# Low parts of 16 weight chunks made by ScalarE and an adding transfer, in one transformer layer

## The chip, the cores and the metric

The kernel runs on one core of a Trainium2 chip. The metric is device microseconds of one execution. A core has TensorE (PE, with its weight loads PEld), VectorE (DVE), ScalarE (ACT), GpSimd (POOL) and SyncE (SP), which run side by side and wait for one another by semaphores, and 16 DMA engines that all of them share. Each engine works through its own instructions in order; so do the queues from which SyncE, ScalarE and GpSimd issue transfers.

## The reference

One layer over a sequence of 256 tokens of width 2048, all in float32: an adaptive scale and shift, windowed attention, a norm, and an MLP of inner width 8192 with another scale, shift and norm. What matters here is the MLP:

```python
u = jnp.square(jax.nn.relu(h @ w1 + b1))
return u @ w2 + b2
```

`w1` is 2048 x 8192 and `w2` 8192 x 2048. The reference multiplies in float32.

## The kernel before

**Split matmuls.** TensorE multiplies in a shorter format (float32r). To keep the accuracy, weights and activations are each split in a high part (the value rounded to that format) and a low part (the value less its high part), and most products are made of three matmuls: high by high, high by low, low by high (`mm3`, lines 543 to 546; line 545 is the one that reads the weight's low part).

**Weights.** A planner (`Stream`) has a list of chunks of 128 x 2048 floats (1 MB). `loads` (line 210) issues their loads from SyncE, in the order of the list, each as soon as one of five `raw` buffers is free. `pump` then makes each chunk's two halves of 128 x 1024 ready, in order: ScalarE casts the raw half to the high part (`wh`, line 277, five buffers), and VectorE subtracts that from the raw half for the low part (`wl`, line 230 in `low`, five buffers). The low parts run one half behind the high parts. When the last low part of a chunk is made, its raw buffer is given back (`freed`), and TensorE's use of a half gives back its `wh` and `wl` (`done`). A chunk with a `use` of its own (the gates) is not split.

**The MLP in four blocks** of 2048 inner columns. In block 0, all of `w2` goes through `ff_out`, one 512-wide output column `c` after the other. In blocks 1 to 3, `ff_mixed` alternates `hidden` (a 128-wide piece of `w1`, activation on ScalarE and VectorE at lines 989 to 996) with `chunk` (output columns 0 and 1 by a product scheme with fewer multiplications, which needs sums of weights and of activations; the latter are `sc`, lines 1004 to 1009). Output columns 2 and 3 then follow in `ff_out`: per column four chunks of `w2`, that is eight halves, each read by twelve matmuls. So in blocks 1 and 2 sixteen halves go through `ff_out` in a row. Beside them VectorE adds up the scheme's results (`gather`, line 1115) and the columns (line 1181) and rescales the residual (`rescale`, lines 1154 and 1155) with rows that GpSimd loads (`gb`, line 1151). Those loads, the gathered column `w`, and the small tiles of the activation share four buffers.

**Order.** In this part of the kernel a scheduler places each engine's instructions, following the order in which the code issues them and when their inputs come free.

Of the kernel before, what the change touches and what calls it, by code (L numbers as in the profile page):

```python
# [14 lines left out]
AF = mybir.ActivationFunctionType  # L15
OP = mybir.AluOpType
# [4 lines left out]
S = 256  # L21
# [27 lines left out]
def hybrid_kernel(ctx: ExitStack, tc: tile.TileContext, a, out: bass.AP):  # L49
    nc = tc.nc  # L50
# [26 lines left out]
    def f32(x):  # L77
        return x.bitcast(F32)
# [97 lines left out]
    class Stream:  # L176
# [4 lines left out]
        def __init__(self):  # L181
            self.q, self.raw = [], []
            self.hs, self.ls, self.src = [], [], []
            self.free, self.home, self.used = [raws] * RAWS + [raws2] * MORE, [], 0
            self.of = []
            self.deep = True
            self.at = self.im = 0
            self.nh, self.nl = NHIGH, NLOW
            self.stop = 0
            self.pace = VECS  # L190
            self.pin = self.behind = False
            self.prev = None
            self.side = {}
            self.parts, self.total, self.j = [], 0, 0
            self.reserve = 0

        def plan(self, src, use=None, kept=0):
            self.q.append((src, use, kept))
            if use is None:
                n = 4 if kept < 0 else 2  # L200
                self.parts.append((self.total, n))
                self.total += n
# [21 lines left out]
        def low(self):  # L224
            n = len(self.ls)
            r, kept, l, last = self.src[n]
            w = r.shape[-1]
            if l is None:
                l = (g4, g4b)[kept - 1](F32R) if kept > 0 else wlp.tile([128, 1024], F32R, name="wl")
            self.pinned(nc.vector.tensor_sub(l[:, :w], r, f32(self.hs[n])[:, :w]))  # L230
            self.ls.append(l)
            if last:
                self.freed(self.of[n])
# [15 lines left out]
        def pump(self, vecs, must=0):  # L249

            while len(self.ls) < must or self.at < len(self.q):
                self.loads()
                n = len(self.hs)
                if len(self.ls) < n - 1 and len(self.ls) - self.used < self.nl or len(self.ls) < min(must, n):
                    self.low()
                    continue
                if self.at >= len(self.q) or self.at == self.stop:
                    return
                assert self.at < len(self.raw)
                src, use, kept = self.q[self.at]  # L260
                if use is not None:
                    if not vecs and n >= must:
                        return
                    vecs = max(vecs - 1, 0)
                    use(self.raw[self.at])
                    self.at += 1
                    self.freed(self.at - 1)
                    continue
                if n >= must and (n - self.used >= self.nh or kept > 0):
                    return  # L270
                j, raw, l = self.j, self.raw[self.at], None
                if kept < 0:
                    h, s, l = self.sums(raw, j)
                else:
                    h = (g4, g4b)[kept - 1](F32R) if kept else whp.tile([128, 1024], F32R, name="wh")
                    s = raw[:, j * 1024:j * 1024 + 1024]
                self.pinned(nc.scalar.copy(h[:, :s.shape[-1]], s))  # L277
                self.hs.append(h)
                self.src.append((s, kept, l, j == (3 if kept < 0 else 1)))
                self.of.append(self.at)  # L280
                self.j = (j + 1) % (4 if kept < 0 else 2)
                self.at += self.j == 0
# [30 lines left out]
    S = Stream()  # L313
# [155 lines left out]
    for g in range(2, G):  # L469
        n = len(ORDER[g])  # L470
# [43 lines left out]
    def plan_out(blk, c):  # L514
        for kg in range(4):
            if blk < BLK - 1:
                m_gf.plan(gf_fill.pop(0))
            S.plan(a["w2"][4 * min(blk, 1) + 2 * max(blk - 1, 0) + (c if blk == 0 else c - 2), kg], None,
                   max(kg - 1, 0) if blk == BLK - 1 and c == 3 else 0)

    first_gf = len(S.q)
    for c in range(4):
        plan_out(0, c)
    for blk in range(1, BLK):
        w1 = [a["w1b"][(blk - 1) * NF + f] for f in range(NF)]
        S.plan(w1[0])
        S.plan(w1[1])
        for i in range(NP):
            if i + 1 < NP:
                S.plan(w1[2 * i + 2])  # L530
            S.plan(a["w2s"][blk - 1, i], None, -1)
            if i + 1 < NP:
                S.plan(w1[2 * i + 3])
        for c in (2, 3):
            plan_out(blk, c)
# [73 lines left out]
    def qkv(g, ch):  # L609

        _, k0, nk = m_mix[g]
        hh, hl = held[g]
        wh, wl = S.main()
        per = 4 // nk
        for ci in range(per):
            p = ch * per + ci
            c = CORD[p]
            go_on, held_back = c in half, ((g, ch), p) in CARRY
            pss = half.pop(c, None) or banks()
            for k2 in range(0, nk, 2):  # L620
                for t in range(NT):
                    for k in (k2, k2 + 1):
                        s = slice(k * 256 + t * 128, k * 256 + t * 128 + 128)
                        mm3(pss[t], hh[:, s], hl[:, s], wh(ci * nk + k), wl(ci * nk + k),
                            k == 0 and not go_on, k == nk - 1 and not held_back)
                S.done()
                if per == 1 and k2 == 0:
                    yield
            if held_back:
                half[c] = pss  # L630
            else:
                evict(c, pss)
            if per == 2 and ci == 0:
                yield
# [36 lines left out]
    for x, (g, c) in enumerate(qk_order):  # L671
        at = ORDER[g].index(c)
# [157 lines left out]
    def project(j, c):  # L830
        wh, wl = S.main()
        oh, ol = oT[j]
        pss = [psa.tile([128, 512], F32, name="pa") for _ in range(NT)]
        last = j == 3 and c == 3
        for t, rs in [(0, range(4)), (1, range(4))] if last else [(t, (r, r + 1)) for r in (0, 2) for t in range(NT)]:
            for r in rs:
                s = slice(t * 512 + r * 128, t * 512 + r * 128 + 128)
                mm3(pss[t], oh[:, s], ol[:, s], wh(r), wl(r), r == 0, r == 3)
            if t == 1 or last:
                S.done(not last)  # L840
            if last:
                add_gated(pss[t], t, c, g1, st)
                sc.append(norm_scalars(st[t]))
                normed(0, t)
            if t == 1 and rs[0] == 0:
                yield
        for t, ps in enumerate(pss):
            if j == 0:
                nc.vector.tensor_add(part(ys, t, c), ps, bo(c))
            elif j < 3:  # L850
                y = part(ys, t, c)
                nc.vector.tensor_add(y, y, ps)
                if j == 2:
                    z = part(xs, t, c)
                    nc.vector.tensor_mul(y, y, g1(c))
                    nc.vector.scalar_tensor_tensor(z, z, ALPHA, y, op0=OP.mult, op1=OP.add)
            elif not last:
                add_gated(ps, t, c, g1, st)
# [21 lines left out]
    for n in range(21):  # L880
        j, i = n // 4, n % 4
# [9 lines left out]
        if n + 1 < len(LATE):  # L891
            w = qkv(*LATE[n + 1])
        else:
            if n == 5:
                ys, bo = [g4b() for _ in range(4)], bias_all(a["bo"], [g4b(), g4b()])
            w = project((n - 5) // 4, (n - 5) % 4)
# [13 lines left out]
        if n == 9:  # L910

            for c in range(4):
                xs[c] = g4()
                i = nc.gpsimd.dma_start(xs[c].rearrange("p (t n) -> p t n", t=NT), a["x"][:, :, 512 * c:512 * c + 512])
# [101 lines left out]
    for n, (kg, fq) in enumerate(W1A):  # L1016
# [4 lines left out]
        for fp in range(2):  # L1021
# [3 lines left out]
            for fi in range(2):  # L1025
                o = ps[:, fi * 256:fi * 256 + 256]
                for k in range(4):
                    w = (fp * 2 + fi) * 4 + k
# [158 lines left out]
    blk = BLK - 1  # L1187
# [130 lines left out]
```

## Time and profile before

| | us |
|---|---|
| median of the runs shown | 1081.9 |
| lowest and highest of 2 | 1081.1, 1082.71 |
| profiled execution | 1085.78 |
| its span | 1084.0 |
| PE busy in it | 1051.5 |
| DVE busy | 926.1 |
| ACT busy | 611.3 |
| POOL busy | 31.0 |

The transfers move 292.70 MB, at a mean of 270 GB/s; 10.50 MB of them go through GpSimd's software queue:

```profile
q1 hardware_dynamic: 39312, 279.85, 66.4%
q0 software_dynamic: 3232, 10.50, 2.8%
```

The columns are packets, MB, and the time that the packets took as a share of 16 engines' span. In the rows of the timeline quoted below stand the start in us, the length, engine, line, operation, output and inputs, and in brackets how long the engine stood idle before and what ended that.

### The profile page before, as it was taken

To read this page: it belongs to the slowest core of one execution; us is meant where nothing else is said; L and a number is where in the kernel's file an instruction comes from. 1 tells how busy PE (TensorE), PEld (TensorE's weight loads), DVE (VectorE), ACT (ScalarE), POOL (GpSimd) and SP (SyncE) were. 2 spreads that over 40 slices of the span, in tenths; PEclk is the share of its full clock that TensorE was granted. 3 is DMA by queue.
4 is the path that set the end of the run, shared out by engine and by line. 5 is a ranking of instruction groups with operands and counts; after the bars stand their busy time and mean duration, and the time that the engine had idled before them with its cause. 6 is when DMAs were issued, how large, how long until landed. Compare 5 with 4: busy or idle time off the path is not lost.

```text
span 1084.0 us, 15688 instructions
## 1 busy us (share of the span) xinstructions
PE 1051.5 (97%) x6026; PEld 846.6 (78%) x6026; DVE 926.1 (85%) x1371; ACT 611.3 (56%) x977; POOL 31.0 (3%) x56
## 2 busy tenths in 40 slices
PE   7899999999999999999999999999999999999995
PEld 5567677666677799988888888888888888888884
DVE  5497899978899877998769889869988977998897
ACT  5333346775773636654357766447767536776640
POOL 1000000001000000000000000000000001000001
PEclk9999999999999999999999999999999999999998
DMA  9999997779976797699835644944564773556632
GB/s 384 426 425 428 425 376 286 277 282 383 368 291 233 322 352 294 236 337 408 342 116 195 215 173 159 385 156 158 192 226 172 273 277 141 183 204 219 246 156 77
DMA packets 43371, 292.70 MB, mean 270 GB/s; under 512 B 5136, under 2 KB 5264, under 8 KB 9504
## 3 DMA queue, kind: packets, MB, share of 16 engines
q1 hardware_dynamic: 39312, 279.85, 66.4%
q0 software_dynamic: 3232, 10.50, 2.8%
q10 hardware_dynamic: 752, 1.35, 0.3%
q8 instruction: 47, 0.77, 0.3%
q14 instruction: 28, 0.23, 0.1%
HBM read 289.57 MB, written 2.11 MB: 269 GB/s over the span
## 4 chain that ended last, share of the span: by engine, by line
PE 81%; DVE 9%; DMA 7%; ACT 2%; issue 1%; SPq 0%; DVEq 0%; ACTq 0%
PE pa L1060 17%; PE pa L544 12%; PE pa L546 12%; PE pa L545 12%; PE pa L1062 8%; DMA raw<-in_modm 4%; PE pa L1033 3%; PE pa L1032 3%; PE pa L1034 3%; DVE wl L230 3%; PE pm L340 2%; DVE g L378 2%; DMA raw<-in_wqkv 1%; DMA raw<-in_modf 1%; PE pa L733 1%
## 5 line engine op out<-in xcount | busy, mean ns | idle before, releaser
L277 ACT CAST wh<-raw 128x1024 fp32r<-128x1024 f32 (+1 forms) x332 | 335.5, 1020 | 288.8 <-PE pa L546 143.6
L230 DVE TENSOR_TENSOR wl<-raw,wh 128x1024 fp32r<-128x1024 f32 (+1 forms) x332 | 387.8, 1181 | 77.0 <-ACT wh L277 71.5
L544 PE MATMUL pa<-wh,g 128*128 128x512 f32 x648 | 258.4, 399 | 5.2 <-ACT g L565 2.1
L546 PE MATMUL pa<-wh,g 128*128 128x512 f32 x648 | 252.8, 393 | 3.7 <-DVE g L567 3.0
L545 PE MATMUL pa<-wl,g 128*128 128x512 f32 x648 | 254.5, 393 | 0.3 <-DVE wl L230 0.3
L1060 PE MATMUL pa<-g,wh 128*128 128x512 f32 x768 | 193.5, 393 | 0.0
L1060 PEld LDWEIGHTS pa<-g,wh 128*128 128x128 f32 x768 | 139.6, 188 | 32.0 <-DVE rl L990 4.5
L544 PEld LDWEIGHTS pa<-wh,g 128*128 128x128 f32 x648 | 121.9, 188 | 41.2 <-issue 7.8
L546 PEld LDWEIGHTS pa<-wh,g 128*128 128x128 f32 x648 | 121.8, 188 | 34.5 <-DVE g L567 6.0
L545 PEld LDWEIGHTS pa<-wl,g 128*128 128x128 f32 x648 | 122.2, 189 | 26.8 <-issue 2.2
L1062 PEld LDWEIGHTS pa<-g,wl 128*128 128x128 f32 x768 | 104.7, 190 | 7.6
L1062 PE MATMUL pa<-g,wl 128*128 128x256 f32 x768 | 107.0, 282 | 0.0
L378 DVE SCALAR_TENSOR_TENSOR g<-raw,cact,g 128x1024 f32<-128x1024 f32 x65 | 82.5, 1278 | 2.4 <-DMA raw<-in_modf 1.9
L1033 PE MATMUL pa<-g,wh 128*128 128x256 f32 x256 | 72.7, 285 | 0.4 <-DVE g L961 0.4
L1032 PE MATMUL pa<-g,wh 128*128 128x256 f32 x256 | 72.5, 286 | 0.0
L1034 PE MATMUL pa<-g,wl 128*128 128x256 f32 x256 | 72.3, 283 | 0.0
L230 DVE TENSOR_TENSOR raw<-raw 128x1024 fp32r<-128x1024 f32 x48 | 58.5, 1221 | 8.6 <-ACT raw L277 7.0
L277 ACT CAST raw<-raw 128x1024 fp32r<-128x1024 f32 x48 | 50.6, 1054 | 13.2 <-PE pm L546 9.8
L340 PE MATMUL pm<-raw,cact 128*32 128x256 f32 (+2 forms) x776 | 47.3, 365 | 8.0 <-DMA raw<-in_modm 4.6
L1032 PEld LDWEIGHTS pa<-g,wh 128*128 128x128 f32 x256 | 48.8, 192 | 1.3 <-issue 0.8
L1033 PEld LDWEIGHTS pa<-g,wh 128*128 128x128 f32 x256 | 49.1, 192 | 0.9 <-DVE g L961 0.8
L1034 PEld LDWEIGHTS pa<-g,wl 128*128 128x128 f32 x256 | 49.1, 192 | 0.0
(220 smaller groups left out, 1205.9 us busy)
## 6 DMA issues: line engine op xcount, KB each, us to landing
raw<-in_w1b SPq DMA_DIRECT2D x48, 1024.0 KB, 5.5
raw<-in_w SPq DMA_DIRECT2D x40, 1024.0 KB, 8.3
raw<-in_modm SPq DMA_DIRECT2D x32, 1024.0 KB, 14.5
raw<-in_modf SPq DMA_DIRECT2D x32, 1024.0 KB, 6.8
raw<-in_wqkv SPq DMA_DIRECT2D x24, 1024.0 KB, 14.1
raw<-in_w2s SPq DMA_DIRECT2D x24, 1024.0 KB, 4.7
raw<-in_modgm SPq DMA_DIRECT2D x16, 1024.0 KB, 7.6
raw<-in_wo SPq DMA_DIRECT2D x16, 1024.0 KB, 7.9
```

The lines of the kernel that those rows point to most:

```text
L230: self.pinned(nc.vector.tensor_sub(l[:, :w], r, f32(self.hs[n])[:, :w]))
L277: self.pinned(nc.scalar.copy(h[:, :s.shape[-1]], s))
L340: i = nc.tensor.matmul(self.ps[32 * j:32 * j + 32, :w], lhsT[j] if type(lhsT) is list else lhsT, rhs[j], start=self.first, stop=stop)
L378: nc.vector.scalar_tensor_tensor(p[:, :e], s, cact[:, kt:kt + 1], p[:, :e], op0=OP.mult, op1=OP.add)
L544: nc.tensor.matmul(ps, xh, wh, start=start, stop=False)
L545: nc.tensor.matmul(ps, xh, wl, start=False, stop=False)
L546: S.prev = nc.tensor.matmul(ps, xl, wh, start=False, stop=stop).ins
L1032: nc.tensor.matmul(o, wh(w, 128), hh, start=new, stop=False)
L1033: nc.tensor.matmul(o, wh(w, 128), hl, start=False, stop=False)
L1034: nc.tensor.matmul(o, wl(w, 128), hh, start=False, stop=end)
L1060: nc.tensor.matmul(ps, wh(k, 128), ff_in(k), start=k == 0, stop=False)
L1062: nc.tensor.matmul(ps[:, :256], wl(k, 128), ff_in(k)[:, :256], start=False, stop=k == NK - 1)
```

## The change

For the chunks of `w2` that blocks 1 and 2 send through `ff_out` (8 each, 16 chunks, 32 halves) the low part is no longer made by VectorE. ScalarE writes the raw half times -1, rounded to the short format, into the `wl` buffer, and a transfer issued by GpSimd adds the raw half to it, read from HBM a second time. `S.adds` names these chunks. In `pump` the low parts of such chunks no longer run one half behind the high parts: a negated copy is issued right after its cast. The other low parts are made as before.

```diff
+            self.adds = {}
...
-            self.pinned(nc.vector.tensor_sub(l[:, :w], r, f32(self.hs[n])[:, :w]))
+            i = self.of[n]
+            if i in self.adds:
+                at = 1024 * (n - self.adds[i])
+                nc.scalar.activation(l, r, AF.Copy, scale=-1.0)
+                nc.gpsimd.dma_start(l, self.q[i][0][:, at:at + 1024], accum_op=OP.add)
+            else:
+                self.pinned(nc.vector.tensor_sub(l[:, :w], r, f32(self.hs[n])[:, :w]))
...
-                if len(self.ls) < n - 1 and len(self.ls) - self.used < self.nl or len(self.ls) < min(must, n):
+                lag = 1 if len(self.ls) < n and self.of[len(self.ls)] not in self.adds else 0
+                if len(self.ls) < n - lag and len(self.ls) - self.used < self.nl or len(self.ls) < min(must, n):
...
+            if blk in (1, 2):
+                S.adds[len(S.q)] = S.total
             S.plan(a["w2"][4 * min(blk, 1) + 2 * max(blk - 1, 0) + (c if blk == 0 else c - 2), kg], None,
```

## The prediction

> **What bounds the kernel now.** I read the page first, for the busy shares and the chain; then the table by stretches around the two places where the changed low parts are used, the waits of TensorE, and the engines there in order of time.
>
> ```profile
> PE 1051.5 (97%) x6026; PEld 846.6 (78%) x6026; DVE 926.1 (85%) x1371; ACT 611.3 (56%) x977; POOL 31.0 (3%) x56
> ...
> PE 81%; DVE 9%; DMA 7%; ACT 2%; issue 1%; SPq 0%; DVEq 0%; ACTq 0%
> ```
>
> TensorE is busy for 97% of the span and carries 81% of the chain of work that ended last. VectorE is busy for 85%, which invites taking work from it; but only what TensorE waits for can shorten the run. So: does TensorE wait where the changed halves are used? The sixteen halves of block 1 feed `ff_out` from the first to the second row here, 676.7 to 724.4 us, where the next block's first matmul follows; those of block 2 come 173 us later. The four rows below them cover both places.
>
> ```profile
> 676.72 0.39 PE L545 MATMUL pa<-wl,g 128*128 128x512 f32 x1
> ...
> 724.42 0.84 PE L1060 MATMUL pa<-g,wh 128*128 128x512 f32 x3
> ...
> 676.00:700.00 24.00, 24.00 (x106) 19.46 (x106) 22.46 (x31) 11.57 (x14) 2.15 (x4) 1.00 0.96 373
> 700.00:724.50 24.50, 24.50 (x110) 20.29 (x109) 15.56 (x17) 9.50 (x9) 0.00 (x0) 1.00 0.62 235
> 849.00:873.00 24.00, 24.00 (x106) 19.50 (x105) 22.42 (x31) 11.48 (x14) 2.15 (x4) 1.00 0.97 378
> 873.00:897.50 24.50, 24.50 (x113) 20.02 (x115) 15.61 (x17) 9.50 (x9) 0.00 (x0) 1.00 0.63 230
> ...
> PE pa L545 <- DVE wl L230: 0.3, 1, 0.3
> ```
>
> Their columns are length, then busy time (and instructions) of PE, PEld, DVE, ACT and POOL, the granted clock, the DMA share and GB/s. PE is busy for all of each stretch, at clock 1.00. The last row, from the waits, is the only wait on a low part that TensorE has in the run: 0.3 us, once. So VectorE, though 22.46 of 24 us busy, is late for nothing here. Little room is left in the DMA engines: 0.96 and 0.97 of them are taken in the first half of each place.
>
> **The change: what goes.** Per place 16 subtractions leave VectorE (two halves for each of 8 chunks, 32 in all).
>
> ```profile
> L230 DVE TENSOR_TENSOR wl<-raw,wh 128x1024 fp32r<-128x1024 f32 x21 | 25.4, 1220 | 8.6 <-ACT wh L277 8.6
> ...
> 705.58 1.06 ACT L277 CAST wh<-raw 128x1024 fp32r<-128x1024 f32 x1 [1.67 <-PE pa L546]
> 708.30 1.06 ACT L277 CAST wh<-raw 128x1024 fp32r<-128x1024 f32 x1 [1.66 <-PE pa L546]
> ```
>
> 16 x 1.220 = 19.5 us of VectorE time per place, 39.0 in all. It buys TensorE nothing beyond that 0.3 us: PE has no idle time here, and its matmuls stay the same in number and form.
>
> **What ScalarE gets.** One pass of 128x1024 per half; the nearest row is the cast of the same size, 1.06 us. The casts follow TensorE every 708.30 - 705.58 = 2.72 us, with 1.66 us idle before each, which covers it: 0 us in the steady part.
>
> **What GpSimd and the DMA engines get.** 16 transfers per place, each 128 x 1024 x 4 bytes = 0.524 MB. No transfer of before adds. The nearest rows are the plain loads (KB each, median us from issue to landing), and below them six microseconds of full engines: 430 GB/s, my ceiling.
>
> ```profile
> raw<-in_w SPq DMA_DIRECT2D x40, 1024.0 KB, 8.3
> ...
> g4b<-row POOLq DMA_DIRECT2D x4, 512.0 KB, 4.6
> g<-in_x POOLq DMA_DIRECT2D x4, 512.0 KB, 11.1
> ...
> gb<-in_lnrow POOLq DMA_DIRECT2D x8, 256.0 KB, 7.4
> ...
> 688.00:694.00 6.00, 6.00 (x28) 4.99 (x27) 5.24 (x8) 3.06 (x3) 0.00 (x0) 1.00 1.02 430
> ```
>
> *Latency, steady part.* There are five `wl` buffers. A half's buffer comes free when TensorE ends the half five back, and is needed four halves later: 4 x 2.72 = 10.9 us. Two ScalarE passes take 2.1, which leaves 8.8 for issue, add and landing. The quickest plain 512 KB land in 4.6 us: hidden, 0 us. At the 11.1 of the `in_x` row the ring would turn in (2.72 + 2.1 + 11.1) / 5 = 3.18 us per half: 16 x 0.46 = 7.4 us per place.
>
> *Latency, first halves.* Here it is not the buffer but the raw chunk that is late, so the lead is shorter:
>
> ```profile
> 670.76 2.01 ACT L277 CAST wh<-raw 128x1024 fp32r<-128x1024 f32 x2 [2.17 <-DMA raw<-in_w]
> ...
> 680.81 2.00 ACT L277 CAST wh<-raw 128x1024 fp32r<-128x1024 f32 x2 [0.85 <-DMA raw<-in_w]
> ...
> 686.57 0.39 PE L545 MATMUL pa<-wl,g 128*128 128x512 f32 x1
> ```
>
> The first half is cast from 670.76; negated by 672.9, it lands at 677.5 with 4.6 us, and TensorE reads it at 676.72: 0.8 late. The third half's raw chunk lands at 680.81; negated by 682.9, it is read at 686.57, a lead of 3.7 us. Against 4.6 that is 0.9 us late, against the 7.4 of `gb` in this very traffic 3.7, against 11.1 it is 7.4. Cover there is none.
>
> *Bytes.* In the 48.5 us from 676 to 724.5 the kernel already moves 24 x 0.373 + 24.5 x 0.235 = 14.7 MB; the ceiling is 48.5 x 0.430 = 20.9, so 6.2 MB are spare (6.2 also at the second place: 24 x 0.378 + 24.5 x 0.230 = 14.7). Sixteen adds bring
> - 8.4 MB if an add costs the engines what a copy of its 0.524 MB does: 2.2 MB too much, 2.2 / 0.430 = 5 us per place;
> - 16.8 MB if it costs twice that, since for each word written it reads two, the raw weight from HBM and the negated high part from `wl`: 10.6 MB too much, 24.7 us;
> - 25.2 MB if both reads and the write count once each: 19 MB too much, 44 us.
>
> I take the middle: an add must read double what a copy reads. Nothing of before tells it from the ends. The Trainium skill, Collectives: The Full Stack, section "The bandwidth ceiling: the fold count and why AG ≠ RS ≠ AR", says that a reducing transfer is slow not by the add but by its two source reads on one read ring, with a measured ratio of 1.93 to the copy. By that ratio the adds weigh 16.2 MB, and a place would lose (16.2 - 6.2) / 0.430 = 23 us; no run here shows it yet.
>
> The low parts' lead of at most 10.9 us is all that covers a lack of 24.7 us of bus time; the rest TensorE waits, from the third half on.
>
> **What is moved.** The four `gb` loads of each place stand in GpSimd's queue between the adds (after the fourth, fifth, eighth and eleventh), each waiting there for a buffer:
>
> ```profile
> 681.64 0.54 POOL L1151 DMA_DIRECT2D gb<-in_lnrow  x1 [1.31 <-DVE sc L1009]
> 697.13 0.54 POOL L1151 DMA_DIRECT2D gb<-in_lnrow  x1 [14.96 <-DVE g4b L1115]
> ```
>
> The longest wait ends at 697; behind it stand the adds for the twelfth half and later, which TensorE reaches at 686.3 + 9 x 2.72 = 710.8: 0 us. The other way round, the `gb` loads come later and VectorE waits for them in its rescaling; what stands behind that (four low parts of the next block, the sums of the second output column) is wanted after 724: 0 us. The raw buffers for SyncE's loads are given back by ScalarE's second pass (2 x 1.06 after the cast begins) in place of the subtraction (1.06 + 1.22): 0 us. On ScalarE two negations come ahead of the steps that make `sc` for the block's last products, and two subtractions leave VectorE ahead of the same steps: 2.1 us later against 2.4 earlier, at most 2 us per place, inside the wait above.
>
> **The sum.** The bus sets the end of each place; the first halves' lateness lies inside that wait. 2 x 24.7 = 49 us. The profiled execution took 1085.8 us (its span 1084.0 and 1.8 around it), 3.9 above the median of 1081.9. So the profile would read 1135, and the median 1131. Its own range reaches from 1108 (half of the second read costs nothing) to 1160 (adds at some 2.7 copies).
>
> **The rivals.**
> 1. *The add hides (not slower by what can be told).* Place: the bus in both stretches. If the second read, from the core's own memory, goes beside the first at no price, 8.4 MB meet 6.2 spare, and loads for the next block can give way. Deciding point: an add lands within 8.8 us. For it: only 0.62 of the engines are taken in the second half of a place. Against it: 0.96 in the first. Price per place from 0.9 (first halves at 4.6 us, bytes given way) to 10 (first halves at 7.4 and 5 of bytes, partly the same): 1084 to 1102; middle 1092.
> 2. *Adds do not overlap one another.* If each takes in turn what a `gb` takes in this traffic, 7.4 us against 2.72 for a half, a place loses 16 x (7.4 - 2.72) = 75 us: 1232; at 4.6 us each 30, and 1142. For it: nothing tells how the engines handle an add. Against it: the raw loads here take 8.3 us at the median and still come at 373 GB/s, so transfers overlap.
> 3. *Freed VectorE helps (faster).* Its 39 us would have to reach TensorE. There is nothing for it but the 0.3 us wait and perhaps half a microsecond of entry per place: 1081. Against it speaks every stretch above.
>
> **How the numbers follow.** Forecast 0.50, first rival 0.27, second 0.20, third 0.03. 2% is 21.6 us (about what a measurement of this kernel can tell from no change): the limit is 1103.5. Faster by that: 0.01. Within: 0.26 of the first rival and 0.02 of the third, 0.28. Slower: 0.71. The range goes from 1084 to 1190: it leaves out the third rival, the quickest of the first (0.05 together) and two thirds of the second (0.13).
>
> **What would show it.** VectorE has 32 subtractions of 128x1024 fewer (39 us); ScalarE 32 passes more at about 1.06 us. The software queue's share of the engines tells the price of an add: 16.8 MB in all at a copy's price are 39 us, 3.6% of the span on top of what is there, 7.2% at double. TensorE waits at L545 for transfers into `wl`, some 25 us per place, the engines full to its end, and for nothing new elsewhere. If there is no such wait and the DMA share of the second half of a place stays below 0.95, the first rival holds; if TensorE waits while the DMA share is low, it is latency or the second rival, and the byte budget is wrong. If TensorE waits for ScalarE's casts, the negations were mis-sized.

## The result and the profile after

| | before | after |
|---|---|---|
| median of the runs, us | 1081.9 | 1143.36 (1142.31 to 1144.41) |
| profiled execution | 1085.78 | 1142.31 |
| its span | 1084.0 | 1140.5 |

The ratio is 1.0568, interval 1.0514 to 1.0622: the change makes the kernel slower by 61.5 us in the medians and by 56.5 in the profiled spans. Lines have moved by 7 to 10 in the changed kernel: 545 is now 555, 1060 is 1070, 1151 is 1161; the new ones are 234 (the negation) and 235 (the adding transfer).

The page of the changed kernel: the busy times, the queues, the chain by engine, and two of the costliest groups.

```profile
PE 1068.3 (94%) x6026; PEld 851.7 (75%) x6026; DVE 890.8 (78%) x1339; ACT 641.1 (56%) x1009; POOL 59.0 (5%) x88
...
q1 hardware_dynamic: 39312, 279.85, 62.9%
q0 software_dynamic: 7840, 27.28, 10.0%
...
PE 71%; DMA 16%; DVE 7%; ACT 3%; issue 2%; POOL 0%; SPq 0%; DVEq 0%; POOLq 0%; ACTq 0%
...
L555 PE MATMUL pa<-wl,g 128*128 128x512 f32 x648 | 260.8, 402 | 41.1 <-DMA wl<-in_w 41.1
...
L235 POOL DMA_DIRECT2D wl<-in_w x32 | 27.8, 868 | 435.3 <-ACT wl L234 209.6
```

VectorE did lose its 32 subtractions: 1371 instructions to 1339, 926.1 us to 890.8. TensorE pays: it stands idle 1140.5 - 1068.3 = 72.2 us where it was 32.5, and is busy 16.8 us longer with the same 6026 matmuls; together the 56.5 of the span. Transfers carry 16% of the chain where it was 7, and 41.1 us of TensorE's idle time are waits at the matmul that reads a low part, all for the adding transfers. The software queue's share gives the price of an add: 10.0% of 1140.5 is 114.0 us of all engines, 2.8% of 1084.0 was 30.4, so 83.7 / 32 = 2.62 us.

The stretches of the first place (columns as before), in the changed kernel:

```profile
676.00:700.00 24.00, 17.62 (x66) 12.92 (x65) 8.28 (x14) 13.63 (x15) 6.90 (x9) 0.93 1.03 330
700.00:724.50 24.50, 17.36 (x60) 12.51 (x60) 4.57 (x8) 9.68 (x11) 4.91 (x6) 0.86 1.05 301
724.50:748.00 23.50, 17.34 (x73) 13.08 (x73) 4.97 (x5) 9.29 (x10) 2.59 (x3) 1.00 1.05 288
748.00:752.00 4.00, 4.00 (x18) 3.31 (x19) 2.56 (x4) 1.52 (x2) 0.00 (x0) 1.00 0.09 33
```

The DMA engines are full (1.03 to 1.05) from 676 to 748, and TensorE, busy for all of such a stretch before, is busy for 17.3 to 17.6 us of each. As soon as the engines fall quiet (0.09), TensorE is busy throughout again. The bytes close: 24 x 0.330 + 24.5 x 0.301 + 23.5 x 0.288 + 4 x 0.033 = 22.2 MB, of which 7.9 are adds (fifteen of the sixteen: the first is used at 675.78 already); the other 14.3 at 430 GB/s are 33 us, fifteen adds at 2.62 are 39, and the sum of 72 stands against 72 us of full engines. (A share above 1 says that packet times overlap a little; a time worked out from shares is some 5% too long for that.)

The chain of waits of the changed kernel, in order of time (start, length), and below it the transfers by their issue (KB each, median us from issue to landing):

```profile
685.87 17.35 DMA wl<-in_w
703.26 0.80 PE pa L555
704.05 0.43 PE pa L556
...
710.71 15.43 DMA wl<-in_w
...
732.90 15.05 DMA wl<-in_w
...
750.78 1.81 PE pa L1070 x8
```

```profile
raw<-in_w SPq DMA_DIRECT2D x40, 1024.0 KB, 8.5
...
wl<-in_w POOLq DMA_DIRECT2D x32, 512.0 KB, 16.0
...
gb<-in_lnrow POOLq DMA_DIRECT2D x8, 256.0 KB, 17.8
```

Within the place the chain goes from one adding transfer to the next, with a few matmuls between. An add takes 16.0 us to land, where the prediction had 8.8 us for issue, add and landing in the steady part. The next block's first matmul starts at 750.78 where it stood at 724.42; the changed kernel had come 3.2 us ahead to this point, so the first place loses 29.6 us. The matmuls before the second place come 26.1 us late and the first one behind it 54.7 (952.16 against 897.43), so the second loses 28.6. The `gb` rows land in 17.8 us instead of 7.4, and VectorE waits up to 11.5 us for one in its rescaling; TensorE waits for none of that.

### The profile page after: what moved, and what is told of

Read it like the earlier page. It is cut to its first block, busy times and chain, and to the rows that moved or that the text cites. A ratio compares the mean times of both kernels' runs of the same rounds, so it can differ in the third digit from the quotient of the medians.

```text
span 1140.5 us, 15777 instructions
## 1 busy us (share of the span) xinstructions
PE 1068.3 (94%) x6026; PEld 851.7 (75%) x6026; DVE 890.8 (78%) x1339; ACT 641.1 (56%) x1009; POOL 59.0 (5%) x88
## 3 DMA queue, kind: packets, MB, share of 16 engines
HBM read 306.35 MB, written 2.11 MB: 270 GB/s over the span
## 4 chain that ended last, share of the span: by engine, by line
PE 71%; DMA 16%; DVE 7%; ACT 3%; issue 2%; POOL 0%; SPq 0%; DVEq 0%; POOLq 0%; ACTq 0%
PE pa L1070 14%; PE pa L555 11%; PE pa L554 11%; PE pa L556 11%; DMA wl<-in_w 9%; PE pa L1072 7%; DMA raw<-in_modm 3%; PE pa L1043 3%; PE pa L1042 3%; PE pa L1044 3%; DMA raw<-in_wqkv 2%; PE pm L348 2%; DVE wl L237 2%; DMA raw<-in_modf 1%; PE pa L743 1%
## 5 line engine op out<-in xcount | busy, mean ns | idle before, releaser
L237 DVE TENSOR_TENSOR wl<-raw,wh 128x1024 fp32r<-128x1024 f32 (+1 forms) x300 | 349.1, 1176 | 86.6 <-ACT wh L285 78.4
L555 PE MATMUL pa<-wl,g 128*128 128x512 f32 x648 | 260.8, 402 | 41.1 <-DMA wl<-in_w 41.1
L554 PE MATMUL pa<-wh,g 128*128 128x512 f32 x648 | 261.1, 404 | 6.0 <-ACT g L575 3.0
L556 PE MATMUL pa<-wh,g 128*128 128x512 f32 x648 | 256.6, 398 | 2.1 <-DVE g L577 2.1
L555 PEld LDWEIGHTS pa<-wl,g 128*128 128x128 f32 x648 | 123.9, 191 | 78.6 <-DMA wl<-in_w 52.6
L554 PEld LDWEIGHTS pa<-wh,g 128*128 128x128 f32 x648 | 123.9, 191 | 42.8 <-issue 7.4
L556 PEld LDWEIGHTS pa<-wh,g 128*128 128x128 f32 x648 | 123.8, 191 | 32.5 <-DVE g L577 5.3
L1072 PEld LDWEIGHTS pa<-g,wl 128*128 128x128 f32 x768 | 104.7, 190 | 7.6
L237 DVE TENSOR_TENSOR raw<-raw 128x1024 fp32r<-128x1024 f32 x48 | 58.7, 1223 | 11.5 <-ACT raw L285 9.5
L285 ACT CAST raw<-raw 128x1024 fp32r<-128x1024 f32 x48 | 50.6, 1054 | 12.1 <-PE pm L556 10.7
L235 POOL DMA_DIRECT2D wl<-in_w x32 | 27.8, 868 | 435.3 <-ACT wl L234 209.6
```

What stands on the lines that cost most here:

```text
L554: nc.tensor.matmul(ps, xh, wh, start=start, stop=False)
L555: nc.tensor.matmul(ps, xh, wl, start=False, stop=False)
L556: S.prev = nc.tensor.matmul(ps, xl, wh, start=False, stop=stop).ins
L1072: nc.tensor.matmul(ps[:, :256], wl(k, 128), ff_in(k)[:, :256], start=False, stop=k == NK - 1)
```

## The experiments

The theory: an add is two reads on the DMA engines, and the engines, nearly full before, set the end. Against it stand a latency (each add simply takes too long for its lead), adds that the engines take one at a time, the ScalarE passes, and lateness of the first halves alone. The ratios are to the kernel before on the same chip; its median was 1081.9 in the first row and 1083 to 1085 in the others.

| kernel | adds per place | median us | ratio, interval | TensorE's waits for adding transfers, us |
|---|---|---|---|---|
| changed kernel | 16 | 1143.36 | 1.0568 [1.0514, 1.0622] | 41.1 |
| copy in place of add | 16 copies | 1111.55 | 1.0257 [1.0225, 1.0289] | 17.7 |
| no transfer | 0 | 1083.41 | 0.9999 [0.9988, 1.0011] | 0 |
| odd chunks | 8 | 1112.64 | 1.0247 [1.0208, 1.0287] | 15.8 |
| chunks of `w1` | 28 in all, elsewhere | 1128.06 | 1.0397 [1.0369, 1.0425] | 28.7 |
| second column | 8 | 1109.78 | 1.0237 [1.0201, 1.0273] | 15.6 |
| first two chunks spared | 12 | 1129.53 | 1.0423 [1.0401, 1.0444] | 29.4 |
| source in SBUF | 16 | 1142.81 | 1.0544 [1.0519, 1.0568] | 35.8 |
| four `wl` in use | 16 | 1144.14 | 1.0551 [1.0518, 1.0584] | 36.9 |
| next loads held | 16 | 1131.33 | 1.0447 [1.0410, 1.0484] | 26.0 |
| last two chunks | 4 | 1093.0 | 1.0089 [1.0062, 1.0117] | 8.0 |
| last two, loads held | 4 | 1085.92 | 1.0021 [1.0006, 1.0036] | 0 |

### A copy in place of the add

```diff
-                nc.gpsimd.dma_start(l, self.q[i][0][:, at:at + 1024], accum_op=OP.add)
+                nc.gpsimd.dma_start(l, self.q[i][0][:, at:at + 1024])
```

The subtraction is left out: the low part of these halves is the raw weight.

> The transfer overwrites the low part with the raw weights instead of adding them, so the low parts are wrong and the subtraction is left out; bytes from HBM, waits and order are those of the changed kernel. Full engines by double reads: a copy takes 1.22 us of all 16 engines against 2.6 for an add, so 16 of them take 19.5 us where 14.3 are spare, 5 us per place and 1092 us in all; transfers into wl still wait in the first halves. The second read costs nothing, or GpSimd's queue is slow whatever it moves: no change, 1143 us. Only latency (first halves late by 4 to 7 us): 1090 to 1097 as well, but then the engines' share in the second half of a place stays near 0.8 to 0.9.

It took 1111.55 us. Only the adding separates it from 1143, so about half of the loss is the price of the add over a copy. But the other half stays, where I had 1092. Its page, its waits, and two of its stretches:

```profile
q0 software_dynamic: 7840, 27.28, 6.9%
```

```profile
PE pa L555 <- DMA wl<-in_w: 17.7, 10, 3.0
```

```profile
680.00:690.00 10.00, 5.17 (x20) 3.62 (x19) 3.26 (x5) 8.35 (x10) 3.73 (x7) 0.95 1.04 411
...
720.00:730.00 10.00, 10.00 (x46) 8.29 (x45) 2.80 (x3) 5.15 (x5) 0.53 (x1) 1.00 0.91 324
```

A copy costs (6.9% x 1109.0 - 30.4) / 32 = 1.44 us, an add 2.62. The ten stops, five per place, all fall in the first halves (to 704 us in the first place), with the engines full at 1.04; in the second half the copies hide. So with the adding gone the first rival's mechanism acts, and still at a higher price than I gave it: the place's own raw loads and the copies share the engines just where the lead is shortest, and the spare of the second half comes too late to help.

### No transfer at all

```diff
-                nc.gpsimd.dma_start(l, self.q[i][0][:, at:at + 1024], accum_op=OP.add)
```

The addition of the raw weights is left out: these low parts stay the negated half.

> The transfer is left out, so the low parts stay at the negated high part; ScalarE's passes and VectorE's relief remain. Full engines: everything lost comes back, 1082 us (1080 to 1084), no wait of TensorE on a low part. ScalarE's passes delay the casts or the entry: 2 us per place more, 1086 us. Freed VectorE helps: below 1081 us by more than the interval.

The ratio is 0.9999 [0.9988, 1.0011]. Its stretches:

```profile
676.00:700.00 24.00, 24.00 (x107) 19.68 (x107) 13.32 (x22) 20.68 (x23) 1.61 (x3) 1.00 1.00 395
700.00:724.50 24.50, 24.50 (x114) 20.44 (x113) 7.91 (x8) 13.99 (x14) 0.00 (x0) 1.00 0.48 173
```

VectorE is busy for 13.3 and 7.9 us where it was 22.5 and 15.6, ScalarE for 20.7 and 14.0 where it was 11.6 and 9.5, and TensorE is busy throughout as it was. The passes on ScalarE cost nothing, the relief of VectorE brings nothing, and the whole loss is the transfers'.

### Half the chunks

```diff
-            if blk in (1, 2):
+            if blk in (1, 2) and kg % 2:
```

> Only every second chunk (8 of 16) is made by ScalarE and an adding transfer, the others by VectorE as before. Full engines: 8 adds take 8 x 2.6 = 21 us where 14.3 are spare, 6.6 us per place, 1095 us; far less than half the loss. Each add costs by itself (serial, or a fixed lateness per half): half the loss, 1112 us. Lateness of the first halves alone: 4 to 5 us per place, 1091 us, with the engines not full at the end of a place.

1112.64 us (its fastest run 1105.64, which is the profiled one): nearly half of the loss, where the spare of a whole place should have covered most of it. A fixed price per add had 1112. The budget of bytes over a whole place is wrong as a forecast, though it closes for the full change. Part of that is the measure of the spare. At 430 GB/s the bytes of before leave 6.2 MB, 14.3 us; but the engines were busy for 0.96 and 0.62 of the two stretches, which leaves 0.04 x 24 + 0.38 x 24.5 = 10.3 us. Eight adds then lack 21 - 10.3 = 10.7 us per place, and the profiled span shows (1103.9 - 1084.0) / 2 = 10.

### As many adds elsewhere

```diff
-            if blk in (1, 2):
-                S.adds[len(S.q)] = S.total
...
+                if blk in (1, 2):
+                    S.adds[len(S.q)] = S.total
                 S.plan(w1[2 * i + 3])
```

The low parts of every second chunk of `w1` in the mixed loops of blocks 1 and 2 are made by adds, those of `w2` by VectorE. These are 14 chunks, 28 adds, fewer than the text below says.

> The same number of adding transfers (16 chunks, 32 halves), but for every second chunk of the first matrix in blocks 1 and 2, and none for the second matrix. There the engines are about half free (0.36 to 0.61 taken), and two adds of 2.6 us meet 8 us of spare time per 16 us. Full engines: they hide, 1082 to 1088 us. Each add costs by itself, wherever it stands: 1143 us. Latency of an add (5.3 us at best) against the short lead of those halves: up to 2.5 us per add, 1100 to 1160 us, with TensorE waiting for wl while the DMA share is well below 1.

It lost 45 us, with the engines far from full on the mean of 20 us. Two stretches of it, below them two shorter ones, and the wait:

```profile
610.00:630.00 20.00, 17.79 (x85) 14.82 (x85) 12.55 (x20) 13.31 (x20) 1.74 (x2) 0.91 0.76 215
630.00:650.00 20.00, 17.82 (x85) 14.87 (x85) 11.46 (x17) 13.13 (x19) 1.74 (x2) 0.91 0.67 196
...
614.00:619.00 5.00, 5.00 (x23) 4.18 (x23) 2.77 (x4) 3.38 (x6) 0.87 (x1) 0.86 0.64 105
620.60:631.60 11.00, 8.16 (x44) 6.67 (x42) 8.27 (x11) 6.55 (x10) 0.87 (x1) 1.00 1.00 321
```

```profile
PE pa L1072 <- DMA wl<-in_w1b: 28.7, 13, 4.7
```

The engines are taken for 0.67 to 0.76 here, the adds land in 5.7 us at the median, and TensorE stops at 13 of the 14 chunks all the same. That looks like a latency with room on the engines, but the two means hide two kinds of adds. The first add of each chunk meets engines that are taken for 0.57 to 0.72 and lands in 5.2 to 5.9 us. The second is issued beside the loads of the next chunks, which fill the engines (1.00 from 620.6 to 631.6 us), and lands in 9.3 to 10.9, but for the earliest. All 13 stops are waits for a second add; the one issued at 620.69 lands at 631.62, after TensorE has waited for 2.90 us. Had those 13 landed in 5.9 us, none would have been late. So here too the cause is full engines, for the ten microseconds or so of one add's flight. A latency alone shows in one stop of the changed kernel: its first add, issued at 670.26, lands in 5.5 us with the engines at 0.70, and TensorE waits 1.79 us for it.

### Adds by themselves

Eight plain loads of 128 x 1024 floats and then eight adds are put behind the last work of the kernel before, each result read by a small VectorE copy.

```diff
...
+    for n, x in enumerate(xs8):
+        nc.gpsimd.dma_start(x, a["w2"][0, 0][:, :1024] if n % 2 else a["w2"][0, 1][:, 1024:])
+    for n, x in list(enumerate(xs8))[::-1]:
+        nc.gpsimd.dma_start(x, a["w2"][0, 2][:, :1024] if n % 2 else a["w2"][0, 3][:, 1024:], accum_op=OP.add)
...
```

> The kernel before, with 8 plain loads and then 8 adding transfers of 0.524 MB each from GpSimd's queue at the very end, into tiles that nothing else uses, with no other traffic. Double reads: the loads come at about 400 GB/s (1.3 us each), the adds at about 200 GB/s by the bytes written (2.6 us each), engines full in both. The add is no dearer than a load: 1.3 us each. Adds one after another, each with its whole landing time: 5.3 us each, engines mostly idle. The time of the whole, some 35 to 60 us above before, says nothing else.

The first stretch below holds loads, the other two adds; under them, from the timeline, two of the copies that wait for the adds one after the other.

```profile
1089.00:1092.00 3.00, 0.00 (x0) 0.00 (x0) 0.00 (x0) 0.00 (x0) 0.00 (x0) 0.50 1.02 376
...
1104.00:1107.00 3.00, 0.00 (x0) 0.00 (x0) 0.15 (x1) 0.00 (x0) 0.00 (x0) 0.50 1.05 208
1107.00:1110.00 3.00, 0.00 (x0) 0.00 (x0) 0.15 (x1) 0.00 (x0) 0.00 (x0) 0.50 1.06 210
```

```profile
1102.80 0.15 DVE L1235 COPY sink<-g 128x1 f32<-128x1 f32 x1 [2.32 <-DMA g<-in_w]
1105.28 0.15 DVE L1235 COPY sink<-g 128x1 f32<-128x1 f32 x1 [2.33 <-DMA g<-in_w]
```

With nothing beside them, in the one execution that was run, adds fill all the engines and end 2.48 us apart: 0.524 MB in 2.48 us is 211 GB/s, as the rows show. A plain load of the same size, at the 376 GB/s of its row, takes 1.4 us. An add is dear by itself; its price is no product of the traffic around it.

### The second column only

```diff
-            if blk in (1, 2):
+            if blk in (1, 2) and c == 3:
```

> Adding transfers only for the 8 chunks of the last output column (the second eight halves of each place), VectorE's subtraction for the first eight. As many adds as with every second chunk, which gave 1112 us. Full engines over the whole place: 21 us of adds against 14.3 spare, 1095 us, and in any case no better than every second chunk. Price per add: 1112 us. Lateness of the first halves, where raw loads, gb loads and adds collide and the lead is 3.7 us: here the lead is 8.8 us and the raw loads are nearly over, so 1083 to 1090 us.

1109.78 us, where the budget of bytes had 1095 and a fixed price per add 1112. The first eight halves, whose lead is short, are spared here, and the loss stays at 26 us: their lateness is not the cause of it. Two stretches of the first place:

```profile
700.00:710.00 10.00, 5.49 (x20) 3.84 (x19) 2.49 (x4) 3.99 (x4) 1.73 (x2) 0.90 1.04 333
...
730.00:740.00 10.00, 9.87 (x51) 8.12 (x51) 5.95 (x8) 4.25 (x5) 0.00 (x0) 1.00 0.14 58
```

In the first place four of these adds are issued from 690.63 on and four behind 700. In the kernel before, the engines were full from 688 to 700 (1.02 and 1.00 in two stretches of 6 us) and had 0.38 x 24.5 = 9.3 us to spare from there; eight adds want 8 x 2.62 = 21. The lack of 11.7 per place is near what the profiled span shows: (1106.5 - 1084.0) / 2 = 11.3. Before 700 only 1 us was free, so this run doesn't tell whether spare ahead of the first add counts.

### All but the first two chunks

```diff
-            if blk in (1, 2):
+            if blk in (1, 2) and (c == 3 or kg > 1):
```

> Adding transfers for all but the first two chunks of each place (12 of 16 chunks). Full engines: 12 x 2.6 = 31 us against 14.3 spare, 17 us per place, 1117 us. Price per add: three quarters of 60, 1128 us. Lateness of the first four halves alone: 1085 to 1095 us.

1129.53 us, where the budget of bytes had 1117 and a fixed price per add 1128. With four adds per place the loss is 9 us, with eight 26 to 29, with twelve 46, with sixteen 61.5: about 4 us of the run for each add more in a place, from the first few on. A late start would have been paid once per place; a price per add repeats.

### The raw half from SBUF

```diff
-                nc.gpsimd.dma_start(l, self.q[i][0][:, at:at + 1024], accum_op=OP.add)
+                nc.gpsimd.dma_start(l, r, accum_op=OP.add)
```

> The adding transfer takes the raw half from its buffer in the core's memory instead of reading it from HBM again; the result is the same, and the raw buffer is held until the add has read it. Price of an add by its two reads, wherever they come from: 1138 to 1150 us (a little more if the later raw loads suffer), HBM bytes as before, about 290 MB. The second trip to HBM is the price: 1100 us or less.

1142.81 us, as the changed kernel. From its page:

```profile
q0 software_dynamic: 7840, 27.28, 10.0%
...
HBM read 289.57 MB, written 2.11 MB: 256 GB/s over the span
```

The kernel reads 16.8 MB less from HBM than the changed one (289.57 against 306.35) and the adds take the same share of the engines, so neither HBM nor the second fetch of the weights is what costs.

### Four low-part buffers in use

```diff
+        S.nl = 4 if blk else NLOW
         for c in (2, 3) if blk else range(4):
...
+        S.nl = NLOW
```

> The changed kernel with low parts made at most four halves ahead in the two places instead of five, so that each add has 2.7 us less from the buffer's release to its use. Full engines: the adds are as many and as dear, and the engines stay full to the end: 1138 to 1150 us. Latency (the ring of buffers turns as fast as an add lands): the ring would turn a quarter slower wherever it is what holds, 8 us or more per place, 1160 us or above.

1144.14 us, 1.0551 against 1.0568: a lead shorter by one half of the weights changes nothing that can be told. The ring is not the bound, which leaves the rate of the adds.

### The next block's loads held back

```diff
-            while len(self.raw) < len(self.q) and self.free:
+            while len(self.raw) < min(len(self.q), self.hold) and self.free:
...
+            S.hold = first_of[blk] + 2
+            S.late.add(S.hold)
...
+            S.stop = first_of[blk]
...
```

In a place SyncE loads no more than two chunks of the next block; the third waits for the place's last matmul. `S.stop` also keeps the next block's halves from being cast while the place's own are issued.

> The changed kernel, with the next block's loads held back in the two places: two of its chunks may be loaded ahead, the third waits for the place's last matmul. Full engines: some 4 MB, 9.5 us of all engines, leave each place to the adds, and the next block starts with two chunks in hand: 1124 us, up to 5 us more per place if that block then waits for its weights. Latency or a price per add: no gain, 1143 us or above.

1131.33 us, 12 us better than the changed kernel. Its waits and three of its stretches:

```profile
PE pa L560 <- DMA wl<-in_w: 26.0, 15, 2.9
```

```profile
690.00:700.00 10.00, 7.39 (x23) 5.30 (x23) 1.90 (x3) 2.28 (x3) 1.77 (x3) 0.83 1.04 332
...
725.00:730.00 5.00, 5.00 (x24) 4.12 (x23) 1.29 (x2) 3.56 (x5) 1.34 (x2) 1.00 1.07 215
730.00:740.00 10.00, 10.00 (x46) 8.27 (x45) 3.68 (x3) 3.95 (x5) 0.87 (x1) 1.00 0.76 150
```

With the loads gone the second half of the place is clean: in the first place TensorE waits for no add after 720.65, though the engines are still full at 725 to 730 (1.07). What is left is lost in the first half, beside loads that the place itself needs. The expected gain was some 19 us and came to two thirds.

### Four adds, and four with the loads held

```diff
-            if blk in (1, 2):
+            if blk in (1, 2) and c == 3 and kg > 1:
```

> Adding transfers only for the last two chunks of the last column (4 of 16 chunks, 4 adds per place), VectorE for the rest. Full engines: 4 x 2.6 = 10.4 us, and from 700 us on some 9.3 us are spare: 1 us per place, 1083 to 1087 us. Price per add (60 us for 32): 1098 us.

1093.0 us, and not nothing. The last four halves of a place have the longest lead and the emptiest engines. The timeline of TensorE:

```profile
715.51 0.50 PE L555 MATMUL pa<-wl,g 128*128 128x512 f32 x1 [0.17 <-DMA wl<-in_w]
...
720.50 0.50 PE L555 MATMUL pa<-wl,g 128*128 128x512 f32 x1 [1.98 <-DMA wl<-in_w]
...
725.54 0.50 PE L555 MATMUL pa<-wl,g 128*128 128x512 f32 x1 [1.98 <-DMA wl<-in_w]
```

The adds arrive 5.0 us apart, twice the 2.48 that they take alone, and TensorE wants one every 2.72. Beside them run loads of the next block that nobody needs yet. If those take every second turn, holding them back must free this kernel: the last run joins both edits.

> Four adds per place (the last two chunks of the last column) and the next block's loads held back as before: both edits together. Full engines, with the adds sharing them with loads that are not urgent: with those gone the four adds meet idle engines, land every 2.6 us instead of every 5.0, and hide: 1082 to 1086 us, no wait for a transfer into wl. If an add is late even on free engines (issue, landing, the ring): 1091 to 1095 us, as without the hold.

1085.92 us, ratio 1.0021 [1.0006, 1.0036]. No wait of TensorE for an add is left, and the transfers by their issue show what an add takes when it is let through:

```profile
wl<-in_w POOLq DMA_DIRECT2D x8, 512.0 KB, 5.6
```

5.6 us against 10.8 in the kernel without the hold and 16.0 in the changed one. This is the first rival come true, for a quarter of the adds and by giving the loads another order; it still doesn't beat the kernel before. No kernel here does.

## Why the prediction came out as it did

**Nothing to gain.** Right: TensorE was busy throughout both places, and the kernel without the transfer measures 0.9999. The third rival is out by the same run.

**Edits at nothing.** ScalarE's passes (1055 ns each by their group, 1.06 forecast) and the raw buffers: right by that run. The row of the groups by line:

```profile
L234 ACT ACTIVATE wl<-raw 128x1024 fp32r<-128x1024 f32 x32 | 33.8, 1055 | 23.1 <-PE pa L555 23.1
```

The `gb` loads behind the adds: late, as said, and nobody on the path waits.

**Double a copy.** Right in kind. The price per add was taken as 2 x 0.524 MB / 430 GB/s = 2.44 us and measured 2.62 by its share in the place and 2.48 by time alone, at a share of 1.05 to 1.06, which is the same price; the copy measured 1.44 and 1.40. The ends are both refuted: a copy's price, and three times it. The Trainium skill, Collectives: The Full Stack, section "The bandwidth ceiling: the fold count and why AG ≠ RS ≠ AR", gives 1.93 for the ratio of a collective's copying step to its reducing one in bandwidth; here it is 2.62 / 1.44 = 1.82 in the place and 2.48 / 1.40 = 1.77 alone, nearer to its rule than to either end. Its reason, the two source reads, fits the run that reads from SBUF, which costs the same; no run here separates a second read from the adding itself.

**Full engines, TensorE waiting at the low part's matmul to the end of the place.** Right: engines at 1.03 to 1.05 until 748, 41.1 us of waits all on L555, no other new wait. But the waits are 20.6 us per place where some 25 were forecast, and the rest of the loss is TensorE's longer busy time, 16.8 us in the run, which the prediction doesn't have. It also says that a lead of up to 10.9 us covers part of the lack, and then rightly takes nothing off for it: the last add sets the end.

**The size.** 24.7 us per place were forecast, 29.6 and 28.6 came. One term is missing from the sum, which ended with the engines: the last low part is there at 747.99, but the next block starts only when its half has been multiplied, at 750.78, 2.8 us later. The remaining 1 to 2 us per place stay open between two terms: the add's price (2.48 us of time for 2.44 is 0.6 per place, 2.62 would be 2.9) and the spare (10.3 us by the engines' busy share for 14.3 by bytes), which together could make more than what lacks. The median lost 61.5 us where the spans show 56.5, since the profiled execution of before lay 3.9 us above its own median and that of after 1.0 below. That is how 1131 became 1143, in the range.

**The second rival** (adds one after another) gives 1142 at its lower price of 4.6 us each, and the time alone could not have told it from the forecast. The adds by themselves do: they end 2.48 us apart, and in the last run they are issued 2.72 us apart and take 5.6 to land, so two are under way together. And full engines are not what it expects. A fixed price per add, though, forecast three of the partial kernels better (1112, 1112 and 1128) than the budget of bytes (1095, 1095 and 1117).

**What was wrong:** the spare. I set the 6.2 MB of the whole place, 14.3 us at 430 GB/s, against the adds. For the partial kernels that forecast far too little loss. Counted in busy shares the spare is 10.3 us, and with it eight adds lack 10.7 us per place, twelve 21.1 and sixteen copies 16 x 1.44 - 10.3 = 12.7; the profiled spans show 10 and 11.3, 22.2, and 12.5. This is worked out from the results, so it is an account and no forecast, and for the sixteen adds it gives 31.6 where the spans show 28.3. The four adds it doesn't fit at all: they want 10.5 us and should have cost next to nothing, and the span lost 4.1 per place. There the mean over a place hides what counts, the spare between an add's issue and its use: loads for later blocks take their turn in it (5.0 us against 2.5 apart), and with these held the loss is gone. The chunks of `w1` show the same. Last, the first halves, which I priced at 0.9 to 7.4 us and put inside the wait, hold all the stops of the kernel with copies: 17.7 us of waits, and 25 of span for both places. So the first rival's 1084 to 1102 was too low: with a copy in place of the add it is 1111.

## What to carry to other kernels

Work is worth taking from an engine only where somebody waits for it; busy 85% is no such sign, and one kernel with the new cost left out (here: no transfer) shows what the relief alone is worth. Price an adding transfer as nearly two copies, and set it against the DMA engines' spare between its issue and its use, not over a whole stage: a mean of 0.76 over 20 us hid that the engines were full just while one add was under way. Where a transfer has a date and others beside it have none, look at their order first: holding loads back was worth 12 us here.

## What the runs showed of the hardware that was not expected

TensorE runs slower after some of its stops. The timeline of the changed kernel after the stop of 3.84 us that ends at 703.26, and the stretch that follows:

```profile
704.28 0.63 PE L554 MATMUL pa<-wh,g 128*128 128x512 f32 x1
704.71 0.63 PE L555 MATMUL pa<-wl,g 128*128 128x512 f32 x1
```

```profile
705.00:707.00 2.00, 2.00 (x6) 1.52 (x6) 1.52 (x3) 0.00 (x0) 0.00 (x0) 0.50 1.05 315
```

The matmuls start 0.43 us apart, where those of the same form before the place start 0.23 apart, and the granted clock is 0.50. In the two places 42 matmuls start that far apart, 42 x 0.20 = 8.4 us, half of the 16.8 us of additional busy time; much of the rest comes at the stops themselves, where the matmul behind a stop is busy for 0.50 us or more. The Trainium skill, TensorE: Matmul & The Clock Gate, section "🔬 Part 1: The HAM clock gate (the "warmup" mystery)", states that the clock halves after an idle window of about 3.4 us and comes back after as much of sustained work. The halving agrees. But in the kernel with the loads held no stop for an add was longer than 2.9 us, and the granted clock is 0.83 in 690 to 700 us: shorter stops are followed by it too. What decides is not shown. In the changed kernel the engines are full all the while, so the slow matmuls probably cost little beyond the wait for the adds. In the kernel with copies they may well have a part in what the stops cost (its granted clock is 0.84 from 690 to 700 us); no run separates the two, and this stays open. With four adds the clock stayed at 1.00 through both places.

The record of an add's issue on GpSimd is also longer: 868 ns by the group of line 235, where the copies in its place take 529. It doesn't hold up the queue by as much: the `gb` load behind the add of 682.85 us begins at 683.39, 0.54 us later.
